# A two-layer trunk on one core: the block products' third phase leaves its chunks at once, and keys, values and queries of layer 1 change places

## The chip, the cores and the metric

One Trainium2 chip, one of its cores. The engines are TensorE (PE; its weight loads are PEld), VectorE (DVE), ScalarE (ACT), GpSimd (POOL) and SyncE (SP), which issues nearly all DMA transfers. The metric is the device time of one execution in microseconds; the profile is of one execution, and its own time stands beside its span below.

## The reference

`x` is 512 x 1024 in fp32, `mem` 256 x 1024. Two layers; each is a mixer, a cross-attention into `mem` with 4 heads of 256, and a gated feed-forward of width 2816 with a causal convolution of width 3. After each of the six steps stands x <- LayerNorm(alpha x + f(x)).

```
for layer in range(2):
    mix = mixer_ab(x, ...) if layer == 0 else mixer_c(x, ...)
    x = layer_norm(alpha * x + mix, ...)
    x = layer_norm(alpha * x + cross_attend(x, mem, wq, wkv, wo), ...)
    x = layer_norm(alpha * x + conv_ffn(x, w_up, conv_w, conv_b, w_down), ...)
```

Layer 0's mixer is a gated half (gelu, a norm, a 128 x 128 mixing of positions) beside a pooling half; layer 1's is `W_out(B * conv3(C * W_in x))`.

## The kernel before

**Numbers.** All matmuls work on fp32 split in two parts: `split` (lines 84 to 87) writes the rounded copy `h` with an ACT cast (L86) and the rest `l` with a DVE subtraction (L87), and `mm3` (226 to 228) multiplies h by h, h by l and l by h into one PSUM bank. A matmul has 128 x 128 stationary and up to 512 moving columns.

**Weights.** `plan` is the list of all weight tiles in the order of use. `Weights.load` fetches up to three tiles ahead with DMAs on SP (L149 or L186) and splits the oldest into a ring of five (`wh`, `wl`); `weights.done()` frees a tile and loads the next, so where `done` stands in the program sets when a load is issued and when its cast and subtraction come in ACT's and DVE's queues. `take` demands the plan's order.

**Activations.** `x` lies as four row blocks of 128 positions (`x0` to `x3`). `to_feat` turns one row block with eight transposes (L366) and splits it into `xT`, the form that the next projection needs. `proj_batch` multiplies several weights with `xT`; given `late`, it computes columns 0 to 255 of all weights first, calls `late` ahead of the last weight (the turning of row blocks 2 and 3), and then columns 256 to 511.

**Block products.** The products that end the mixers (`ab_w_out`, `c_w_out`) and the feed-forwards (`ffn_w_down`, five of its six groups) use seven block products in place of eight, on 2 x 2 blocks of both sides (`Blocks`, `fast_product`, lines 370 to 454). POOL forms the sums of weight blocks (L162, L169 to L171). The first phase multiplies A11, A12 and S1, the second S2 and S4, the third S3 (onto the bank X) and A22 (bank Z). Between them DVE adds the banks to the row blocks of `x` (L381) and PE goes on into the same banks, so a matmul of the next phase waits for the add before it. In the last group the statistics (L486) and the norms (`normalise`, L336 to L341, with a power on POOL, L338) stand between. In the third phase the order is A22 of half 0, S3 of half 0, S3 of half 1, A22 of half 1; its weights are freed only in half 1.

**Around.** The last product before a use of `mem` calls `prepare`: the norm's rows, the slots of the next `xT`, and with `ahead` the loading and splitting of `mem` (`load_mem`, L91). The keys (`proj_k`) come next, beside the norms: whole in layer 0, with the turning of row blocks 0, 1 ahead of head 2 and 2, 3 ahead of head 3. In layer 1 heads 0 and 1 come ahead of `mixer_c`, heads 2 and 3 after `c_w_out`. `attend` then computes the queries (four weights at once, then one each), loads `mem` again, and interleaves scores (softmax: L701 to L711), values and turned probabilities (L719). The tiles for all of it come from a ring of 12 (`act`).

The order of each engine's queue is not the program's alone: a scheduler places instructions within it. The listings below show that order.

Of the kernel before, what the change touches and what calls it, by code (L numbers as in the profile page):

```python
# [20 lines left out]
HEADS = 4  # L21
# [16 lines left out]
def kernel(ctx: ExitStack, tc: tile.TileContext, a: dict, out: bass.AP):  # L38
    nc = tc.nc
# [73 lines left out]
    for layer in range(2):  # L113
        if layer == 0:
            plan += [("ab_w_v", i) for i in range(4)] + [("ab_w_f", i) for i in range(4)] + [("pool_w",)]
            plan += [("ab_w_f", i) for i in range(4, 8)]
            plan += fast_plan("ab_w_out", 0, 0, 4)
            plan += [("xa_wk", layer, i) for i in range(8)]
        else:
            plan += [("xa_wk", layer, i) for i in range(4)]  # L120
            plan += [("c_w_in", i) for i in range(24)]
            plan += fast_plan("c_w_out", 0, 0, 4)
            plan += [("xa_wk", layer, i) for i in range(4, 8)]
        plan += [("xa_wq", layer, i) for i in range(8)]
        plan += [("xa_wv", layer, n, i) for n in range(2) for i in range(4)]
# [244 lines left out]
    def fast_product(act, name, layer, i0, first, norm=None):  # L370

        halves = (0, 1)
        seen = set()

# [51 lines left out]
        for p in halves:  # L428
            add(p, 1, X[p])
        for p in halves:  # L430
            add(p, 1, Y[p])
            stat(p, 1)
            if norm:
                norm[1](p)
        ts = [[weights.take(w, name, layer, i0 + i, i0 + top(i)) for i in firsts] for w in ("t3t3", "t4t4")]
        for p in halves:

            for k in (1, 0) if p == 0 else (0, 1):
                for i in range(n):
                    if k == 0:  # L440
                        mul(X, Blocks.S3, i, p, ts[0][i // 2], i % 2, True)
                    else:
                        mul(Z, Blocks.A22, i, p, ts[1][i // 2], i % 2)
                    if p and (i % 2 or i == n - 1):
                        weights.done()
                if k == 0:
                    add(p + 2, 1, X[p])
                    stat(p + 2, 1)
                    add(p + 2, 0, X[p])
                else:  # L450
                    add(p + 2, 0, Z[p])
            stat(p + 2, 0)
            if norm:
                norm[1](p + 2)

    def residual_norm(groups, wname, ln, layer, last=False, hooks={}, ahead=None):

# [7 lines left out]
        for gi, (make, k0, k1) in enumerate(groups):  # L465
# [25 lines left out]
            def prepare():  # L491
# [3 lines left out]
                if ahead:  # L495
                    ahead()

            if fast:
                fast_product(act, wname, wi, k0 // 2, gi == 0, (stat, norm, prepare))
                return xT, lambda: [to_feat(xT, t) for t in (0, 1)], lambda: [to_feat(xT, t) for t in (2, 3)]  # L500

            for n in range(2):
                if n == 0 or not final:
# [28 lines left out]
                    norm(t)  # L532
                weights.done(len(chunks))

        return xT, None, lambda: [to_feat(xT, t) for t in (2, 3)]


    def mixer_ab(xT):
# [61 lines left out]
        last = None  # L600
        for gi in range(4):
            (ps,) = proj_batch([("ab_w_f", 4 + gi)], xT)
            if gi < 2:
                pool_block(2 * gi)
                pool_block(2 * gi + 1)
            if gi == 1:
                weights.done()
            if last:
                gate_block(*last)
            ut = tmp()  # L610
            nc.scalar.activation(ut, ps, AF.Gelu_apprx_tanh)  # L611
            last = gi, ut
        gate_block(*last)
        return y
# [10 lines left out]
    def mixer_c(xT, late):  # L625
        y = Blocks()
        for m in range(KD):
            ps = proj_batch([("c_w_in", m * 3 + i) for i in range(3)], xT, late if m == 0 else None)
# [11 lines left out]
    def mem_at(t, i, k, c):  # L640
        return t[k // 4][i][:, (k % 4) * MEM + c.start : (k % 4) * MEM + c.stop]

    def proj_k(layer, mem, hooks={}, heads=range(HEADS)):
        full = slice(0, MEM)
        kT = [duo() for _ in heads[::2]]
        for h in heads:
# [10 lines left out]
            i = (h - heads[0]) // 2  # L657
            split(kT[i][0][:, c], kT[i][1][:, c], ps)
        return kT

    def proj_v(layer, mem, n):
        v = duo()
        ps = [ps_tile() for _ in range(2)]
        for k in range(KD):
            if k % 2 == 0:
# [12 lines left out]
    def attend(layer, xT, late, kT):  # L678

        q, o = Act(8), Act(8)  # L680
        for m0, m1 in ((0, 4), (4, 5), (5, 6), (6, 7), (7, 8)):
            ps = proj_batch([("xa_wq", layer, m) for m in range(m0, m1)], xT, late if m0 == 0 else None)
            for m in range(m0, m1):
                split(q.h(m), q.l(m), ps[m - m0])
        mem = load_mem()
        es, pT, v = {}, {}, {}

        def scores(h):
            es[h] = []
# [42 lines left out]
        scores(0)  # L732
        v[0] = proj_v(layer, mem, 0)
        turn(0)
        scores(1)
        values(0)
        v[1] = proj_v(layer, mem, 1)
        turn(1)
        scores(2)
        values(1)  # L740

        def second():
            turn(2)
# [36 lines left out]
        weights.load_beside(2 if k < 2 else 1, a["xT"][k], xT.tiles[k])  # L780
    weights.done(RING - 4)

    early = late = None
    mem = []

    def load_ahead():
        mem.append(load_mem())
# [1 line left out]
    for layer in range(2):  # L789
        if layer == 0:  # L790
            y = mixer_ab(xT)
            xT, early, late = residual_norm([(lambda: y, 0, 8)], "ab_w_out", "ln_mix", layer, ahead=load_ahead)
            kT = proj_k(layer, mem.pop(), {2: early, 3: late})
            late = None
        else:
            kT = proj_k(layer, mem.pop(), {1: early}, (0, 1))
            y = mixer_c(xT, late)
            xT, early, late = residual_norm([(lambda: y, 0, 8)], "c_w_out", "ln_mix", layer, ahead=load_ahead)
            kT += proj_k(layer, mem.pop(), {3: early}, (2, 3))
        o, hooks = attend(layer, xT, late, kT)  # L800
        xT, early, late = residual_norm([(lambda: o, 0, 8)], "xa_wo", "ln_xa", layer, hooks=hooks)
        up = [(lambda m0=m0, m1=m1, xT=xT, late=late: ffn_up(layer, xT, late, m0, m1), m0, m1) for m0, m1 in FFN_GROUPS[layer]]
        xT, early, late = residual_norm(up, "ffn_w_down", "ln_ffn", layer, layer == 1, ahead=None if layer else load_ahead)


# [73 lines left out]
```

## Time and profile before

| | |
|---|---|
| median of 3 runs | 1362.38 us (1360.58 to 1364.28) |
| the profiled execution's own time | 1363.97 us |
| its span, first to last instruction | 1362.2 us |
| mean granted TensorE clock | 0.989 of full |
| PE, DVE, ACT, POOL busy | 98%, 67%, 38%, 16% |
| DMA | 171.58 MB, mean 126 GB/s |

A matmul's row in the profile lasts from its start to the modelled end of its pipeline (389 ns at 512 columns), while the next starts sooner; how many start in a window tells the pace. A wait is put down to the instruction that released it last: `PE ps L226 <- DVE x L381` is time in which a matmul written on line 226 waited for a DVE instruction of line 381. The granted clock is that of TensorE in the window: 1.00 is full, 0.50 half.

### The profile page before, as it was taken

Reading aid. Unit: us, or ns where it says so; the run is one execution under the profiler, and the core shown is the slowest. Engines: PE = TensorE matmul, PEld = TensorE weight load, DVE = VectorE, ACT = ScalarE, POOL = GpSimd, SP = SyncE. Lnnn points to the kernel's source line nnn. Section 1 sums busy time; section 2 is a strip of 40 time slices with the busy share of each in tenths; the row PEclk is TensorE's granted clock in tenths of the full one; section 3 lists DMA queues with packets and bytes.
Section 4 is the critical chain, followed back from the end, with each engine's and each line's share of the span. In section 5 each row is a group of like instructions: output and inputs, shape, how many; then the busy total and the mean of one; then the engine's idle time right before and its main releaser. Section 6 shows DMA issues by size and latency. Waiting matters only on the chain. (4 is left out here: it accounts for less than half of the span.)

```text
span 1362.2 us, 16656 instructions
## 1 busy us (share of the span) xinstructions
PE 1328.3 (98%) x6541; PEld 1125.0 (83%) x6541; DVE 916.6 (67%) x1167; ACT 521.9 (38%) x667; POOL 217.2 (16%) x176
## 2 busy tenths in 40 slices
PE   9988999999999999999899999899999999999997
PEld 7867988888888888888888888888898888888886
DVE  6898746586676676579754579556577586577446
ACT  5443435324443443344333334245234334343330
POOL 1251000010240220142000151000010320141001
PEclk9989999999999999999899999899999999999998
DMA  8526634122354344236333335443123354236301
GB/s 312 162 93 203 214 111 151 48 78 85 101 171 131 93 133 160 86 105 213 124 109 100 101 124 189 153 138 111 61 78 102 100 185 124 88 114 218 107 0 62
DMA packets 50910, 171.58 MB, mean 126 GB/s; under 512 B 6032, under 2 KB 6160, under 8 KB 50832
## 3 DMA queue, kind: packets, MB, share of 16 engines
q1 hardware_dynamic: 49104, 164.23, 37.4%
q0 software_dynamic: 1728, 6.29, 1.3%
q8 instruction: 51, 0.84, 0.3%
q14 instruction: 27, 0.22, 0.0%
HBM read 168.40 MB, written 2.10 MB: 125 GB/s over the span
## 5 line engine op out<-in xcount | busy, mean ns | idle before, releaser
L87 DVE TENSOR_TENSOR wl<-raw,wh 128x1024 fp32r<-128x1024 f32 (+1 forms) x279 | 353.2, 1274 | 231.9 <-ACT wh L86 228.8
L228 PE MATMUL ps<-act,wl 128*128 128x512 f32 (+1 forms) x1340 | 484.5, 362 | 4.8 <-DVE wl L87 4.8
L226 PE MATMUL ps<-act,wh 128*128 128x512 f32 (+1 forms) x1340 | 484.6, 362 | 3.1 <-DVE rs L337 2.1
L227 PE MATMUL ps<-act,wh 128*128 128x512 f32 (+1 forms) x1340 | 484.6, 362 | 0.0
L86 ACT CAST wh<-raw 128x1024 fp32r<-128x1024 f32 (+1 forms) x279 | 290.0, 1042 | 480.7 <-PE ps L227 289.9
L228 PEld LDWEIGHTS ps<-act,wl 128*128 128x128 f32 x1340 | 255.3, 191 | 43.2 <-DVE wl L87 5.5
L226 PEld LDWEIGHTS ps<-act,wh 128*128 128x128 f32 x1340 | 255.1, 191 | 41.6 <-issue 2.3
L227 PEld LDWEIGHTS ps<-act,wh 128*128 128x128 f32 x1340 | 255.5, 191 | 37.8
L226 PE MATMUL ps<-wh,act 128*128 128x512 f32 (+1 forms) x656 | 257.6, 394 | 8.9 <-ACT tmp L611 4.6
L227 PE MATMUL ps<-wl,act 128*128 128x512 f32 (+1 forms) x656 | 255.3, 389 | 0.0
L228 PE MATMUL ps<-wh,act 128*128 128x512 f32 (+1 forms) x656 | 255.0, 389 | 0.0
L226 PEld LDWEIGHTS ps<-wh,act 128*128 128x128 f32 x656 | 124.4, 190 | 38.4 <-DVE x L381 5.7
L228 PEld LDWEIGHTS ps<-wh,act 128*128 128x128 f32 x656 | 123.9, 189 | 25.5
L227 PEld LDWEIGHTS ps<-wl,act 128*128 128x128 f32 x656 | 124.1, 189 | 25.0 <-DVE wl L87 0.2
L338 POOL TENSOR_TENSOR rs<-rs,mhalf 128x1 f32<-128x1 f32 x28 | 39.7, 1418 | 512.0 <-DVE rs L337 512.0
L162 POOL TENSOR_TENSOR raw<-raw,raw 128x512 f32<-128x512 f32 x27 | 38.6, 1431 | 454.7 <-DVE wl L87 376.9
L86 ACT CAST act<-ps 128x512 fp32r<-128x512 f32 x104 | 57.1, 591 | 84.8 <-PE ps L366 63.3
L87 DVE TENSOR_TENSOR act<-ps,act 128x512 fp32r<-128x512 f32 x104 | 67.8, 684 | 22.4 <-ACT act L86 22.4
L381 DVE SCALAR_TENSOR_TENSOR x<-x,ps 128x512 f32<-128x512 f32 x112 | 72.3, 676 | 10.4 <-PE ps L228 10.4
L87 DVE TENSOR_TENSOR act<-blocks,act 128x768 fp32r<-128x768 f32 (+1 forms) x54 | 71.8, 1341 | 10.6 <-ACT act L86 10.6
L86 ACT CAST act<-blocks 128x768 fp32r<-128x768 f32 (+1 forms) x54 | 48.9, 942 | 66.2 <-DVE blocks L277 66.2
L623 DVE SCALAR_TENSOR_TENSOR tmp<-ps,convw,tmp 128x511 f32<-128x511 f32 x88 | 65.6, 746 | 1.6
(80 smaller groups left out, 830.3 us busy)
## 6 DMA issues: line engine op xcount, KB each, us to landing
raw<-in_ffn_w_up SPq DMA_DIRECT2D x88, 512.0 KB, 3.7
raw<-in_ffn_w_down SPq DMA_DIRECT2D x63, 512.0 KB, 3.6
raw<-in_c_w_in SPq DMA_DIRECT2D x24, 512.0 KB, 3.6
raw<-in_xa_wk SPq DMA_DIRECT2D x16, 512.0 KB, 4.6
raw<-in_xa_wq SPq DMA_DIRECT2D x16, 512.0 KB, 4.3
raw<-in_xa_wv SPq DMA_DIRECT2D x16, 512.0 KB, 3.7
raw<-in_xa_wo SPq DMA_DIRECT2D x16, 512.0 KB, 4.4
raw<-in_ab_w_out SPq DMA_DIRECT2D x12, 512.0 KB, 3.8
```

The lines of the kernel that those rows point to most:

```text
L86: nc.scalar.copy(h, src)
L87: nc.vector.tensor_sub(l, src, h.bitcast(F32))
L162: nc.gpsimd.tensor_sub(both("t1"), w1[:, half[0]], w0[:, half[0]])
L226: nc.tensor.matmul(ps, lh, rh, start=start, stop=False, skip_group_check=more)
L227: nc.tensor.matmul(ps, lh, rl, start=False, stop=False, skip_group_check=more)
L228: nc.tensor.matmul(ps, ll, rh, start=False, stop=stop, skip_group_check=more)
L338: nc.gpsimd.tensor_tensor(rs, rs, mhalf, op=ALU.pow)
L381: nc.vector.scalar_tensor_tensor(z, z, scale, ps, op0=ALU.mult, op1=ALU.add)
L623: nc.vector.scalar_tensor_tensor(dst[:, s:], src[:, : S - s], tap(2 - s), dst[:, s:], op0=ALU.mult, op1=ALU.add)
```

## The change

The third phase of `fast_product` now runs S3 for both halves, chunk by chunk, and then A22; each chunk is freed as soon as it is used. The norm's callback has two parts: `ahead` (loading `mem`) is called before the second phase and the rows after it. The norms of row blocks 0 and 1 are called at the chunks of S3, that of block 2 at the end, and that of block 3 becomes the first of three hooks that the caller places. Layer 1 computes all four heads of keys ahead of `mixer_c` with these hooks at heads 1, 2 and 3; after `c_w_out` it computes the values (both halves) with the hooks in them, and `attend` begins with the queries, six of them, then scores(0), query 6, scores(1), query 7. Neither `c_w_in` nor the queries of layer 1 runs in halves any longer, and `mem` is loaded four times instead of five. In `mixer_ab` the gelu of a gate batch is written right after its projection.

```
-            plan += [("xa_wk", layer, i) for i in range(4)]
+            plan += [("xa_wk", layer, i) for i in range(8)]
...
         Z = [ps_tile() for _ in halves]
+        if norm:
+            norm[2]()
         for i in range(n):
             b = weights.take("t2b22", name, layer, i0 + i, i0 + i // 2 * 2, i0 + top(i // 2 * 2))
...
         if norm:
-            norm[2]()
+            norm[3]()
...
-            if norm:
-                norm[1](p)
-        ts = [[weights.take(w, name, layer, i0 + i, i0 + top(i)) for i in firsts] for w in ("t3t3", "t4t4")]
+        for i in firsts:
+            t3 = weights.take("t3t3", name, layer, i0 + i, i0 + top(i))
+            if norm and i < 4:
+                norm[1](i // 2)
+            for j in range(i, top(i)):
+                for p in halves:
+                    mul(X, Blocks.S3, j, p, t3, j - i, True)
+            weights.done()
+        for m in (1, 0):
+            for p in halves:
+                add(p + 2, m, X[p])
+                if m:
+                    stat(p + 2, 1)
+        for i in firsts:
+            t4 = weights.take("t4t4", name, layer, i0 + i, i0 + top(i))
+            for j in range(i, top(i)):
+                for p in halves:
+                    mul(Z, Blocks.A22, j, p, t4, j - i)
+            weights.done()
         for p in halves:
...
+            add(p + 2, 0, Z[p])
             stat(p + 2, 0)
-            if norm:
-                norm[1](p + 2)
+        if norm:
+            norm[1](2)
...
             (ps,) = proj_batch([("ab_w_f", 4 + gi)], xT)
+            ut = tmp()
+            nc.scalar.activation(ut, ps, AF.Gelu_apprx_tanh)
             if gi < 2:
...
-            ut = tmp()
-            nc.scalar.activation(ut, ps, AF.Gelu_apprx_tanh)
             last = gi, ut
...
+            for m in range(6):
+                queries(m, m + 1)
+            scores(0)
+            queries(6, 7)
+            scores(1)
+            queries(7, 8)
+            o = Act(8)
+            turn(0)
+            scores(2)
+            values(0)
+            turn(1)
+            values(1)
...
-            kT = proj_k(layer, mem.pop(), {1: early}, (0, 1))
-            y = mixer_c(xT, late)
...
-            kT += proj_k(layer, mem.pop(), {3: early}, (2, 3))
...
+            kT = proj_k(layer, mem.pop(), dict(zip((1, 2, 3), left)))
+            y = mixer_c(xT)
+            xT, left = residual_norm([(lambda: y, 0, 8)], "c_w_out", "ln_mix", layer, ahead=load_ahead)
+            v = {0: proj_v(layer, mem[0], 0, {4: left[0]}), 1: proj_v(layer, mem.pop(), 1, {0: left[1], 6: left[2]})}
+        o, hooks = attend(layer, xT, kT, v)
```

**ACT at the end of the first mixer.** `blocks` are the gate's blocks, written by DVE; the last L611 (L607 in the change) is the gelu of the last gate batch. Before:

```order
L86 CAST wh_714<-raw_577 128x1024
L611 ACTIVATE tmp_736<-ps_680 128x512
L86 CAST act_728<-blocks_676 128x768
L86 CAST act_733<-blocks_676 128x1024
L86 CAST wh_770<-raw_635 128x1024
L611 ACTIVATE tmp_783<-ps_738 128x512
```

And now:

```order
L86 CAST wh_714<-raw_577 128x1024
L607 ACTIVATE tmp_718<-ps_680 128x512
L86 CAST act_730<-blocks_678 128x768
L86 CAST act_735<-blocks_678 128x1024
L86 CAST wh_770<-raw_635 128x1024
L607 ACTIVATE tmp_774<-ps_738 128x512
```

The last gelu stands behind the same three casts in both.

**DVE from the first to the second phase of `ab_w_out`, layer 0.** `x_113` to `x_116` are the row blocks 0 to 3, `act_937` and `act_942` the two parts of `mem` (before, `act_1017` is the first of them), `wl` low halves of weights. Before:

```order
L381 SCALAR_TENSOR_TENSOR x_115<-x_115,ps_809 128x512
L87 TENSOR_TENSOR wl_918<-raw_862,wh_917 128x1024
L87 TENSOR_TENSOR wl_922<-row_709,wh_921 128x1024
L381 SCALAR_TENSOR_TENSOR x_116<-x_116,ps_810 128x512
L486 BN_STATS stats_803<-x_113 128x6
L486 BN_STATS stats_804<-x_114 128x6
L87 TENSOR_TENSOR wl_950<-row_835,wh_949 128x1024
L87 TENSOR_TENSOR act_1017<-raw_1015,act_1017 128x1024
L87 TENSOR_TENSOR wl_968<-raw_712,wh_967 128x1024
L381 SCALAR_TENSOR_TENSOR x_113<-x_113,ps_811 128x512
L87 TENSOR_TENSOR wl_986<-raw_838,wh_985 128x1024
L381 SCALAR_TENSOR_TENSOR x_114<-x_114,ps_812 128x512
```

And now:

```order
L382 SCALAR_TENSOR_TENSOR x_116<-x_116,ps_810 128x512
L87 TENSOR_TENSOR wl_918<-raw_862,wh_917 128x1024
L87 TENSOR_TENSOR wl_922<-row_709,wh_921 128x1024
L491 BN_STATS stats_803<-x_113 128x6
L491 BN_STATS stats_804<-x_114 128x6
L87 TENSOR_TENSOR act_937<-raw_935,act_937 128x1024
L87 TENSOR_TENSOR act_942<-raw_940,act_942 128x1024
L87 TENSOR_TENSOR wl_960<-row_835,wh_959 128x1024
L87 TENSOR_TENSOR wl_978<-raw_712,wh_977 128x1024
L382 SCALAR_TENSOR_TENSOR x_113<-x_113,ps_811 128x512
L87 TENSOR_TENSOR wl_996<-raw_838,wh_995 128x1024
L382 SCALAR_TENSOR_TENSOR x_114<-x_114,ps_812 128x512
```

The fourth row block's add moved ahead of two weights; both parts of `mem` now stand ahead of the adds of X (`ps_811`, `ps_812`), with the first weights of S3 and A22.

**ACT at the same place of the first feed-forward's last group.** `wh_4958` and `wh_4962` are weights of the second phase and of S3, `act_5058` and `act_5063` (now `act_4978` and `act_4983`) are `mem`. Before:

```order
L86 CAST wh_4936<-raw_4872 128x1024
L86 CAST wh_4958<-raw_4903 128x1024
L86 CAST wh_4962<-row_4784 128x1024
L86 CAST wh_4990<-row_4876 128x1024
L86 CAST act_5058<-raw_5056 128x1024
L86 CAST wh_5008<-raw_4787 128x1024
L86 CAST wh_5026<-raw_4879 128x1024
L86 CAST act_5063<-raw_5061 128x1024
```

And now:

```order
L86 CAST wh_4936<-raw_4872 128x1024
L86 CAST act_4978<-raw_4976 128x1024
L86 CAST act_4983<-raw_4981 128x1024
L86 CAST wh_4958<-raw_4903 128x1024
L86 CAST wh_4962<-row_4784 128x1024
L86 CAST wh_5000<-row_4876 128x1024
L86 CAST wh_5018<-raw_4787 128x1024
L86 CAST wh_5036<-raw_4879 128x1024
```

Both parts of `mem` moved ahead of the second phase's last weight and of S3's first.

More of the change, by code (lines that the diff above doesn't have):

```diff
@@ L119 @@
         else:
-            plan += [("xa_wk", layer, i) for i in range(4)]
+            plan += [("xa_wk", layer, i) for i in range(8)]
             plan += [("c_w_in", i) for i in range(24)]
             plan += fast_plan("c_w_out", 0, 0, 4)
-            plan += [("xa_wk", layer, i) for i in range(4, 8)]
-        plan += [("xa_wq", layer, i) for i in range(8)]
-        plan += [("xa_wv", layer, n, i) for n in range(2) for i in range(4)]
+        wq = [("xa_wq", layer, i) for i in range(8)]
+        wv = [("xa_wv", layer, n, i) for n in range(2) for i in range(4)]
+        plan += wv + wq if layer else wq + wv
         plan += [("xa_wo", layer, n, i) for n in range(2) for i in range(4)]
@@ L494, in prepare @@
                 xT = Wide(KD)
-                if ahead:
-                    ahead()
             if fast:
-                fast_product(act, wname, wi, k0 // 2, gi == 0, (stat, norm, prepare))
-                return xT, lambda: [to_feat(xT, t) for t in (0, 1)], lambda: [to_feat(xT, t) for t in (2, 3)]
+                fast_product(act, wname, wi, k0 // 2, gi == 0, (stat, norm, ahead or (lambda: None), rows))
+                return xT, (lambda: norm(3), lambda: [to_feat(xT, t) for t in (0, 1)], lambda: [to_feat(xT, t) for t in (2, 3)])
             for n in range(2):
@@ L533, in residual_norm @@
                 weights.done(len(chunks))
-        return xT, None, lambda: [to_feat(xT, t) for t in (2, 3)]
+        return xT, (lambda: [to_feat(xT, t) for t in (2, 3)],)
     def mixer_ab(xT):
@@ L623, in conv3, with mixer_c @@
             nc.vector.scalar_tensor_tensor(dst[:, s:], src[:, : S - s], tap(2 - s), dst[:, s:], op0=ALU.mult, op1=ALU.add)
-    def mixer_c(xT, late):
+    def mixer_c(xT):
         y = Blocks()
         for m in range(KD):
-            ps = proj_batch([("c_w_in", m * 3 + i) for i in range(3)], xT, late if m == 0 else None)
+            ps = proj_batch([("c_w_in", m * 3 + i) for i in range(3)], xT)
             p, cv = tmp(), tmp()
@@ L641, in mem_at, with proj_k @@
         return t[k // 4][i][:, (k % 4) * MEM + c.start : (k % 4) * MEM + c.stop]
-    def proj_k(layer, mem, hooks={}, heads=range(HEADS)):
+    def proj_k(layer, mem, hooks={}):
         full = slice(0, MEM)
-        kT = [duo() for _ in heads[::2]]
-        for h in heads:
+        kT = [duo() for _ in range(2)]
+        for h in range(HEADS):
             if h in hooks:
@@ L656, in proj_k, with proj_v @@
             c = slice((h % 2) * 512, (h % 2) * 512 + 512)
-            i = (h - heads[0]) // 2
-            split(kT[i][0][:, c], kT[i][1][:, c], ps)
+            split(kT[h // 2][0][:, c], kT[h // 2][1][:, c], ps)
         return kT
-    def proj_v(layer, mem, n):
+    def proj_v(layer, mem, n, hooks={}):
         v = duo()
@@ L664, in proj_v @@
         for k in range(KD):
+            if k in hooks:
+                hooks[k]()
             if k % 2 == 0:
@@ L676, in proj_v, with attend, queries @@
         return v
[L678 to L682, printed above, removed]
+    def attend(layer, xT, kT, v):
+        q = Act(8)
+        def queries(m0, m1):
+            ps = proj_batch([("xa_wq", layer, m) for m in range(m0, m1)], xT)
             for m in range(m0, m1):
                 split(q.h(m), q.l(m), ps[m - m0])
-        mem = load_mem()
-        es, pT, v = {}, {}, {}
+        es, pT = {}, {}
         def scores(h):
@@ L730, in values @@
                 split(o.h(2 * h + d), o.l(2 * h + d), ps)
[L732 to L740, printed above, removed]
+        if v is None:
+            for m in range(8):
+                queries(m, m + 1)
+            o, v, mem = Act(8), {}, load_mem()
+            scores(0)
+            v[0] = proj_v(layer, mem, 0)
+            turn(0)
+            scores(1)
+            values(0)
+            v[1] = proj_v(layer, mem, 1)
+            turn(1)
+            scores(2)
+            values(1)
+        else:
+            for m in range(6):
+                queries(m, m + 1)
+            scores(0)
+            queries(6, 7)
+            scores(1)
+            queries(7, 8)
+            o = Act(8)
+            turn(0)
+            scores(2)
+            values(0)
+            turn(1)
+            values(1)
         def second():
@@ L781 @@
     weights.done(RING - 4)
-    early = late = None
-    mem = []
+    mem, left = [], None
     def load_ahead():
@@ L791 @@
             y = mixer_ab(xT)
-            xT, early, late = residual_norm([(lambda: y, 0, 8)], "ab_w_out", "ln_mix", layer, ahead=load_ahead)
-            kT = proj_k(layer, mem.pop(), {2: early, 3: late})
-            late = None
-        else:
-            kT = proj_k(layer, mem.pop(), {1: early}, (0, 1))
-            y = mixer_c(xT, late)
-            xT, early, late = residual_norm([(lambda: y, 0, 8)], "c_w_out", "ln_mix", layer, ahead=load_ahead)
-            kT += proj_k(layer, mem.pop(), {3: early}, (2, 3))
[L800 to L803, printed above, removed]
+            xT, left = residual_norm([(lambda: y, 0, 8)], "ab_w_out", "ln_mix", layer, ahead=load_ahead)
+            kT = proj_k(layer, mem.pop(), dict(zip((1, 2, 3), left)))
+            v = None
+        else:
+            kT = proj_k(layer, mem.pop(), dict(zip((1, 2, 3), left)))
+            y = mixer_c(xT)
+            xT, left = residual_norm([(lambda: y, 0, 8)], "c_w_out", "ln_mix", layer, ahead=load_ahead)
+            v = {0: proj_v(layer, mem[0], 0, {4: left[0]}), 1: proj_v(layer, mem.pop(), 1, {0: left[1], 6: left[2]})}
+        o, hooks = attend(layer, xT, kT, v)
+        xT, left = residual_norm([(lambda: o, 0, 8)], "xa_wo", "ln_xa", layer, hooks=hooks)
+        up = [(lambda m0=m0, m1=m1, xT=xT, late=left[0]: ffn_up(layer, xT, late, m0, m1), m0, m1) for m0, m1 in FFN_GROUPS[layer]]
+        xT, left = residual_norm(up, "ffn_w_down", "ln_ffn", layer, layer == 1, ahead=None if layer else load_ahead)
 def _layout(inputs):
```

16 lines of the change are left out of this document (1 added, 15 removed).

## The prediction

> **What bounds the kernel now.** I read the page first, then the waits of the matmul engine, then windows cut along the steps of the granted clock.
>
> ```profile
> span 1362.2 us, 16656 instructions
> PE 1328.3 (98%) x6541; PEld 1125.0 (83%) x6541; DVE 916.6 (67%) x1167; ACT 521.9 (38%) x667; POOL 217.2 (16%) x176
> PE ps L228 <- DVE wl L87: 4.8, 3, 1.8
> PE ps L226 <- ACT tmp L611: 4.6, 1, 4.6
> PE ps L226 <- DVE x L381: 4.3, 8, 1.5
> PE ps L366 <- DVE act L87: 3.9, 4, 1.4
> PE ps L226 <- DVE rs L337: 2.1, 1, 2.1
> PE ps L366 <- DVE rs L337: 2.1, 1, 2.1
> ```
>
> TensorE sets the time: it is busy in 98% of the span and no other engine reaches 70%. So only two kinds of gain exist: fewer or cheaper matmuls, and fewer stalls of PE. The waits (line: total us, times, longest) name the stalls: a late low half of a weight (L87), the last gelu of the first mixer (L611), the residual adds of the block products (L381), and the norms with their turned copies (L337 and L366). The listed ones sum to 21.8 us. A stall has a second price, which the windows show (us, PE busy and instructions, granted clock, DMA share, GB/s):
>
> ```profile
> 81.75:85.16 3.41, 0.00 (x0) 1.00 0.83 303
> 85.16:88.58 3.42, 2.78 (x7) 0.50 0.01 2
> 88.58:91.99 3.41, 3.41 (x10) 0.50 0.06 10
> 102.23:105.64 3.41, 1.63 (x6) 1.00 0.83 290
> 129.53:132.94 3.41, 1.59 (x14) 1.00 0.01 2
> 132.94:136.36 3.42, 3.42 (x18) 0.50 0.65 182
> 136.36:139.77 3.41, 3.41 (x31) 1.00 0.31 125
> 658.60:662.00 3.40, 0.88 (x7) 1.00 0.81 299
> 662.00:665.40 3.40, 2.00 (x9) 0.50 0.44 160
> 665.40:668.85 3.45, 3.45 (x19) 0.50 0.22 33
> 839.50:842.90 3.40, 2.00 (x17) 1.00 0.00 0
> 853.15:856.56 3.41, 0.36 (x1) 1.00 0.84 297
> 856.56:859.97 3.41, 2.39 (x10) 0.50 0.76 253
> 859.97:863.40 3.43, 3.43 (x18) 0.50 0.87 220
> ```
>
> The clock moves in steps of 3.41 us. At full clock, a window with 1.59 us of work or less was followed by one at 0.50, one with 1.63 or 2.00 was not; at half clock, 2.00 and 2.39 kept it there. A full window at half clock does 18 matmuls of 256 columns where 136.36 to 139.77 does 31, so it costs 3.41 x 13/31 = 1.4 us; I count 1.5. Counted over starts of matmuls, loss sits in four places: the last gelu of the first mixer (about 8 us, with two half windows), the output product and keys of layer 0 (8.4), the end of the first feed-forward with keys and first batch of layer 1 (9.2), and the output product, keys and queries of layer 1 (10.0). In the last two, the stalls alone are about 6.
>
> **Half batches made whole: -2.2 us.** The first batch of c_w_in (3 weights) and of the queries of layer 1 (4) run in halves of 256 columns before. The change runs them whole: 168 pairs of 256-column matmuls become 168 of 512 columns.
>
> ```profile
> 674.00:684.00 10.00, 10.00 (x85) 1.00 0.16 54
> 690.00:750.00 60.00, 60.00 (x267) 1.00 0.30 93
> ```
>
> A window counts the matmul that hangs over its edge, so 85 in 10 us is 0.119 us each and 267 in 60 us is 0.2255. Two halves cost 0.238, a whole 0.2255, and 168 x 0.0125 = 2.1. The spacing of single starts (0.120 and 0.227) gives 2.2, which I take; counts off by one give 1.8 to 2.7.
>
> **Gelu ahead: 0.** The gelu of the last gate batch is written ahead of the gate work, but on ACT it still stands behind the two casts of the blocks, as the first order listing shows.
>
> ```profile
> 82.53 1.78 ACT L86 CAST act<-blocks 128x768 fp32r<-128x768 f32 x2 [4.52 <-DVE blocks L277]
> 85.16 0.59 ACT L611 ACTIVATE tmp<-ps 128x512 f32<-128x512 f32 x1
> ```
>
> ACT sat idle 4.52 us until the blocks came, while this gelu's input was long done, and PE waits for the gelu to free its bank. Nothing of that queue changes, so the 4.6 us wait and the two half windows stay. Bounds: 0.6 (the 0.59 us of one gelu) either way.
>
> **Memory split ahead, third phase by chunks.** memT's two loads now stand before the second phase, and their casts and subtractions stand ahead of the weights that the second phase still needs.
>
> ```profile
> 615.61 6.72 SPq L186 DMA_DIRECT2D raw<-in_xa_wk  x4
> 620.14 1.05 ACT L86 CAST wh<-raw 128x1024 fp32r<-128x1024 f32 x1 [3.18 <-POOL raw L170]
> 621.30 1.06 ACT L86 CAST wh<-row 128x1024 fp32r<-128x1024 f32 x1
> 623.00 1.21 DVE L87 TENSOR_TENSOR wl<-row,wh 128x1024 fp32r<-128x1024 f32 x1
> 624.13 0.67 DVE L381 SCALAR_TENSOR_TENSOR x<-x,ps 128x512 f32<-128x512 f32 x1
> raw<-in_xa_wk SPq DMA_DIRECT2D x2, 512.0 KB, 4.4
> ```
>
> At the end of the first feed-forward the slots that xa_wk's loads took from 615.61 become memT's. The first two of these took 4.4 us to land (the last row, over 615 to 619), the second issued about 617.7, so memT lands near 620.2 and 622.1. ACT waits for it: cast one, cast two from 622.1 to 623.1, the two weights to 625.2 instead of 622.4. DVE's subtractions follow and the fourth residual add ends near 627.1 instead of 624.8. PE waits there today 0.2 to 0.4 us; now about 2.6, **+2.3**. Queued behind it on DVE stand two statistics, memT's subtractions and two weights, then the adds of X that the third phase needs; PE is late by as much, so no second stall follows here. In return the keys of layer 1 run as four whole heads, 192 matmuls of 256 columns = 23 us, beside the last norms; the stalls at 645 to 648 and 658 to 665 and both half windows go, and about 0.8 us is left at the turning of the fourth row block. Loss 9.2 before, 3.4 to 3.5 after: **-5.7**.
>
> The same pattern stands at the output product of layer 1.
>
> ```profile
> 815.00 1.06 ACT L86 CAST wh<-raw 128x1024 fp32r<-128x1024 f32 x1 [4.08 <-POOL raw L170]
> 818.49 0.67 DVE L381 SCALAR_TENSOR_TENSOR x<-x,ps 128x512 f32<-128x512 f32 x1
> ```
>
> That add would end at 821.1 instead of 819.16, a stall of 2.6 instead of 0.8. The values (96 matmuls of 512 columns, 96 x 0.227 = 21.8 us) then cover the norms. What is late next is the turned copy of the fourth row block: its subtractions are queued behind three weights on DVE (1.21 us each), and the first query waits some 2.3. Loss 10.0 before, 5.3 after: **-4.7**.
>
> In layer 0 it is worse covered, since X's adds come sooner after.
>
> ```profile
> 101.63 2.10 SPq L186 DMA_DIRECT2D raw<-in_xa_wk  x4
> 102.00 1.05 ACT L86 CAST wh<-row 128x1024 fp32r<-128x1024 f32 x1 [0.23 <-PE ps L228]
> 107.86 0.67 DVE L381 SCALAR_TENSOR_TENSOR x<-x,ps 128x512 f32<-128x512 f32 x1
> raw<-in_xa_wk SPq DMA_DIRECT2D x4, 512.0 KB, 5.2
> ```
>
> memT takes the first two of the four issues at 101.63 and lands 3.6 to 4.7 us later (their median is 5.2). The casts end near 107.7 and the two weights near 109.7. DVE's list in the second order listing then gives: weights to 111.0, statistics to 112.3, memory to 114.6, two weights to 117.0, first X add to 117.6, one weight, second X add near 119.3. PE is ready for S3, which now comes first in the third phase, at 115.2: it waits 2 to 2.5 and then about 1.0. Before, A22 stood there and covered both adds; 6 matmuls per chunk of A22 (1.4 us) no longer do. Against that go the fourth add's 0.7 at 107.7, the stall and half window at 129.5 to 136.4, and 1.2 near 151. Loss 8.4 before, 6.1 after: **-2.3**.
>
> **Attention of layer 1: +1.7.** The order now ends turn(1), values(1), where scores(2), 24 matmuls or 2.9 us, stood between.
>
> ```profile
> L707 ACT ACTIVATE tmp<-ps,mx 128x256 f32<-128x256 f32 x32 | 14.8, 478 | 5.8 <-DVE mx L702 5.7
> L86 ACT CAST act<-ps 128x512 fp32r<-128x512 f32 x104 | 57.1, 591 | 84.8 <-PE ps L366 63.3 <-PE ps L228 21.4
> ```
>
> Values(0) with turn(1) take 12 x 0.227 + 8 x 0.11 = 3.6 us after scores(2). ACT in that time does a cast once half of values(0) is there (1.4 + 0.6), four exponentials (4 x 0.45 by their starts), a cast, and the cast that values(1) needs: 5.0 and some handing over. PE waits 1.4 to 1.7; below, 0 if ACT takes the cast first.
>
> **The other four products: +0.3.** S3 first puts their X adds (0.67 us) on the edge of the path; each gains or loses up to 0.3. One memT load and split fewer lies beside matmuls: 0.
>
> Sum: -2.2 + 0 - 2.3 - 5.7 - 4.7 + 1.7 + 0.3 = -12.9 without half windows. Four new stalls of 2.3 to 3.5 us can each starve a window. A stall of 2.6 leaves a window at most 1.6 us of work in 7 of 10 positions against the 3.41 us grid ((3.41 + 2.6 - 2 x 1.8)/3.41). So two to three half windows at 1.5 add about 4: **-9**. The profiled run took 1363.97 us, 1.8 more than its span and 1.6 more than the median, so the sum gives 1355 for that run and 1353.4 against the median of 1362.38.
>
> The Trainium skill ("TensorE: Matmul & The Clock Gate", Part 1) says that the clock falls back after about one whole idle window of 3.4 us. By that rule no new stall would cost clock and the time would be 1349.5. This trace disagrees: the window from 129.53 still held 1.59 us of work, and the next ran at 0.50.
>
> **Rivals.**
> 1. The waits only move. Each of the three products also gets two half windows after its stall, as 658 to 669 shows, and the first queries get one: 7 x 1.5 = 10.5 on -12.9, 1360. For it: 0.88 us of work, in a window with pauses on both sides of a short burst, brought two. Against: the new stalls come as one pause.
> 2. Slower: memT comes late. ACT takes its casts in order, so each us that memT lands later moves three products. Landings here run from 3.5 to 6.6 us. Say each pair lands d later, and the stalls of 2.6 + d then empty a whole window and bring two half windows each (+3.0): -12.9 + 3(d + 3.0) is a loss of 0.3% (4.1 us) from d = 2.7. At d = 3 it is +5.1, 1367.5. DMA share 0.83 in the windows beside speaks for late landings, the 4.4 us for xa_wk in the same slots against.
> 3. No wait at the adds: memT lands before ACT needs it. Then 2 x 2.3 and 3 us go from the sum with their half windows: about 1342.
> 4. The gelu does get ahead: 4.6 + 3.0 more, 1345.8. The order speaks against it.
> 5. The change doesn't do what it says: norms and turned copies still hold up the first query and first batch, only the halves and layer 0's part are left, 1358 to 1359.
>
> **How the numbers follow.** Forecast, with 2 or 3 half windows, 1350 to 1357: 0.66. Rival 1: 0.12, rival 2: 0.04, rival 3: 0.07, rival 4: 0.04, rival 5: 0.07. About 0.3%, 4.1 us, is what a measurement can tell from no change, so faster means below 1358.3. The forecast, rivals 3 and 4, and about half of rivals 5 and 1 are faster: 0.85; same 0.10; slower 0.05. The range 1345 to 1360 leaves out rivals 2 and 3 and parts of 1.
>
> **What the changed profile would show.** The waits L337 at the first batch and first query are gone; the wait for L611 is still 4.6 us; the waits for the residual adds grow to some 9 us in all, with one of 2 to 3 us in each of the three products; a new one of 1.5 us at the end of layer 1's values. PE has 168 instructions fewer. Wrong would be: no residual add above 1 us (rival 3), or a wait above 4 us at one with memT ahead of it on ACT (rival 2).

## The result and the profile after

The changed kernel takes 1351.72 us, the median of 4 runs (1350.42 to 1352.94), against 1363.09 for the kernel before beside it. The ratio is 0.9919 (95% interval 0.9900 to 0.9938); on a second chip, beside other kernels, it was 0.9901 (0.9882 to 0.9921). So it is 0.8 to 1.0% faster, 11 to 13 us. The profiled execution took 1352.71 us, with a span of 1350.9.

The page of the changed kernel, and then its waits of PE (line: total us, times, longest):

```profile
span 1350.9 us, 16327 instructions
...
PE 1321.7 (98%) x6373; PEld 1110.2 (82%) x6373; DVE 915.6 (68%) x1165; ACT 519.5 (38%) x665; POOL 219.9 (16%) x176
```

```profile
PE ps L226 <- DVE x L382: 10.3, 8, 3.1
PE ps L226 <- ACT tmp L607: 4.6, 1, 4.6
PE ps L226 <- ACT act L86: 1.2, 1, 1.2
...
PE ps L226 <- DVE act L87: 0.7, 1, 0.7
PE ps L226 <- DVE tmp L595: 0.4, 1, 0.4
PE ps L366 <- DVE act L87: 0.3, 1, 0.3
```

PE has 168 instructions less and is still 98% busy. The waits for a weight's low half (4.8 us) and for the norms (2.1 and 2.1) are gone, those for turned copies fell from 3.9 to 0.3. The waits for the residual adds (now line 382) grew from 4.3 to 10.3, one of 1.2 us is new at the end of layer 1's values, and the gelu's 4.6 us stayed.

Where the time went is seen when each start of a matmul is compared with the spacing of undisturbed ones (0.2267 us at 512 columns, 0.120 at 256, 0.109 at 128) and the excess summed by stretch:

| stretch (times of the kernel before) | before | after | forecast, half windows apart |
|---|---|---|---|
| first mixer's end, 78 to 99 | 7.9 | 7.4 | 7.9 |
| output product and keys of layer 0, 99 to 160 | 8.4 | 7.0 | 6.1 |
| last product of the first feed-forward to first batch of layer 1, 600 to 690 | 9.2 | 5.4 | 3.5 |
| output product, values, queries of layer 1, 800 to 890 | 10.1 | 4.6 | 5.3 |
| attention of layer 1, 890 to 1000 | 0.2 | 1.8 | 1.9 |
| the other four products | 1.6 | 2.5 | 1.9 |
| all of the span | 40.3 | 31.2 | |

The excess fell by 9.2 us and the span by 11.3; the 2.1 between them is what 168 whole matmuls cost less than 336 halves at these spacings.

The windows of the granted clock, after the change, on the grid of its own changes (at 103.27, 106.69, 625.51 and 628.92, whole multiples of 3.413 us apart; us, PE busy, clock, DMA share, GB/s):

```profile
622.10:625.51 3.41, 0.88 (x4) 1.00 0.76 244
625.51:628.92 3.41, 3.41 (x10) 0.50 0.70 232
820.07:823.49 3.42, 2.76 (x13) 1.00 0.73 253
823.49:826.90 3.41, 1.77 (x8) 1.00 0.73 229
826.90:830.31 3.41, 3.41 (x17) 1.00 0.78 267
```

Two stalls of nearly one length, 2.7 and 2.5 us. The first lies inside one window, leaves 0.88 us of work in it, and the next window runs at half clock. The second is cut by a border, the worse of its windows still has 1.77, and the clock stays. The Trainium skill ("TensorE: Matmul & The Clock Gate", Part 1) asks for an idle window of 3.4 us before the clock falls; 0.88 us of work did not prevent it here.

### The profile page after: what moved, and what is told of

It reads as the page before. It is cut to its first block, busy times and chain, and to the rows that moved or that the text cites. A ratio compares the mean times of both kernels' runs of the same rounds, so it can differ in the third digit from the quotient of the medians.

```text
span 1350.9 us, 16327 instructions
## 1 busy us (share of the span) xinstructions
PE 1321.7 (98%) x6373; PEld 1110.2 (82%) x6373; DVE 915.6 (68%) x1165; ACT 519.5 (38%) x665; POOL 219.9 (16%) x176
## 5 line engine op out<-in xcount | busy, mean ns | idle before, releaser
L226 PE MATMUL ps<-act,wh 128*128 128x512 f32 (+1 forms) x1284 | 473.1, 369 | 0.8 <-DVE act L87 0.7
L227 PE MATMUL ps<-act,wh 128*128 128x512 f32 (+1 forms) x1284 | 473.0, 368 | 0.1
L228 PE MATMUL ps<-act,wl 128*128 128x512 f32 (+1 forms) x1284 | 472.9, 368 | 0.0
L226 PEld LDWEIGHTS ps<-act,wh 128*128 128x128 f32 x1284 | 242.1, 189 | 41.8 <-DVE act L87 1.9
L227 PEld LDWEIGHTS ps<-act,wh 128*128 128x128 f32 x1284 | 242.2, 189 | 40.3 <-DVE act L87 0.4
L228 PEld LDWEIGHTS ps<-act,wl 128*128 128x128 f32 x1284 | 242.2, 189 | 39.8
L226 PE MATMUL ps<-wh,act 128*128 128x512 f32 (+1 forms) x656 | 258.4, 395 | 15.3 <-DVE x L382 10.3
L228 PE MATMUL ps<-wh,act 128*128 128x512 f32 (+1 forms) x656 | 256.2, 391 | 0.0
L228 PEld LDWEIGHTS ps<-wh,act 128*128 128x128 f32 x656 | 124.4, 190 | 26.0
L338 POOL TENSOR_TENSOR rs<-rs,mhalf 128x1 f32<-128x1 f32 x28 | 43.1, 1539 | 483.0 <-DVE rs L337 483.0
```

Source lines behind the costliest of these rows:

```text
L226: nc.tensor.matmul(ps, lh, rh, start=start, stop=False, skip_group_check=more)
L227: nc.tensor.matmul(ps, lh, rl, start=False, stop=False, skip_group_check=more)
L228: nc.tensor.matmul(ps, ll, rh, start=False, stop=stop, skip_group_check=more)
L338: nc.gpsimd.tensor_tensor(rs, rs, mhalf, op=ALU.pow)
```

## The experiments

My theory was the sum of the prediction: the moved work of layer 1 covers the norms, the chunks freed at once keep the keys' start free, and the price is that memT's casts, first in ACT's queue, hold up the fourth residual add. The rival that grew out of the first runs: VectorE's queue is the scarce thing in these stretches, so that what counts is whether it has something to do while PE waits. The runs were taken on three chips, with the kernel before beside them each time. A ratio is known to between 0.001 and 0.002, which is 1 to 3 us, so a difference of that size between two of them decides nothing by itself.

**memT after the second phase (e1).**

```
-        if norm:
-            norm[2]()
         for i in range(n):
             b = weights.take("t2b22", ...)
...
         if norm:
             norm[3]()
+            norm[2]()
```

> The changed kernel, with memT loaded and split after the second phase again, as before the change; everything else stays. My theory: memT's two casts on ACT, which wait for their data ahead of the second phase's last weight, make the waits at the fourth residual add (2.7 us at 624.8, 2.5 at 825.1) and part of the ones at S3 in layer 0 (0.6 and 0.9). These fall to 0.4, 0.8 and about 0.3, and the half window after 625 goes: 2.3 + 1.7 + 1.2 + 1.5 = 6 to 7 us less than the changed kernel, about 1345. Rival: it is the early memory that keeps the keys' start free, and with it late the waits of the keys for a weight's low half (1.98, 1.74, 1.57 us before the change) come back: then the two cancel, 1351 to 1354, with PE waiting at L228 for DVE L87 at the start of the keys.

Measured: 0.9937 of the kernel before (0.9921 to 0.9954), 2 to 5 us above the changed kernel (0.9901 and 0.9919 in its two measurements). The waits of PE in it:

```profile
PE ps L226 <- DVE x L382: 6.6, 10, 3.0
PE ps L366 <- DVE act L87: 5.9, 3, 2.7
```

The two waits for the fourth add shrank as my theory said, from 2.7 and 2.5 to 0.4 and 0.7 us, and still the kernel was slower: nearly 3 us each are lost in front of the transposes beside the keys of both layers, and 1.8 at the first query. That is neither my theory nor the wait that its rival named (L228 at the keys). VectorE's busy time points to a reason. In the kernel before, in the changed one and in e1, in this order (us, DVE busy and instructions, clock, DMA share, GB/s):

```profile
622.00:640.00 18.00, 14.87 (x20) 1.00 0.77 265
640.00:668.00 28.00, 28.00 (x38) 0.89 0.39 131
```

```profile
622.00:640.00 18.00, 16.28 (x21) 0.91 0.78 262
640.00:668.00 28.00, 27.56 (x38) 1.00 0.50 152
```

```profile
622.00:640.00 18.00, 14.07 (x18) 1.00 0.74 251
640.00:668.00 28.00, 27.56 (x38) 1.00 0.55 171
```

From 640 to 668, the stretch of the norms, VectorE is full, or all but full, in all three. In the 18 us ahead of it, it idles 3.1 us before the change, 1.7 in the changed kernel and 3.9 in e1. My reading: work on memory done there fills VectorE time that would be lost, so what PE pays at the add it gets back at the transposes. These rows alone do not prove it. Taken from 606 on, the three idle 3.2, 4.0 and 4.2 us, since VectorE in the changed kernel stands still 2.25 us ahead of the fourth add. And from 600 to 690 the excess in e1 is 5.2 us, against 5.4 and 3.0 in the two profiles of the changed kernel. The clear loss lies in layer 0, from 99 to 160: 9.7 against 7.0 and 5.0.

**The old third phase (e2).** In the changed kernel, A22 of half 0 again goes first, and the chunks are freed in half 1; the norms of row blocks 0 and 1 stand ahead of the phase, and that of block 3 stays with the caller.

```
-        for i in firsts:
-            t3 = weights.take("t3t3", ...)
...
+        ts = [[weights.take(w, ...) for i in firsts] for w in ("t3t3", "t4t4")]
+        for p in halves:
+            for k in (1, 0) if p == 0 else (0, 1):
...
+                    if p and (i % 2 or i == n - 1):
+                        weights.done()
```

> The changed kernel with the third phase in the old order (A22 of half 0, S3 of both halves, A22 of half 1, weights freed in the second half only); memT stays early, keys, values and queries stay moved. My theory: freeing the chunks at once is what took away the waits of the keys for a weight's low half (1.98, 1.74, 1.57 us), so with the old order they come back, and with them at least one half window (1.5): +5 to +7; the waits at S3 (0.6 and 0.9 in layer 0, 1.0 in the last block product) go: -2.5. Sum +3 to +4.5, about 1355.5. Rival: the keys' start was freed by the early memory and the moved norms, not by the chunks; then only the gain is left, 1349.

Measured: 0.9893 (0.9876 to 0.9909), as fast as the changed kernel or 1 to 3 us faster. The waits at S3 in layer 0 are gone, the keys wait 0.7 us once for a low half, and none of the three waits of 1.6 to 2 us came back:

```profile
PE ps L226 <- DVE x L382: 8.0, 6, 2.6
...
PE ps L226 <- ACT wh L86: 0.5, 1, 0.5
PE ps L228 <- DVE wl L87: 0.5, 1, 0.5
```

The rival holds: leaving the chunks at once, the part that gives the change its name, brings no gain that these runs can tell.

**Both undone (e9).** The old third phase and memory after the second phase, so that of the change the moved keys, values and queries, the whole batches and the gelu are left.

> The changed kernel with both parts of the block product undone: memT after the second phase and the old third phase. What is left of the change is the moved keys, values and queries of layer 1, the whole batches and the gelu. If the memory and the third phase matter only through VectorE's queue, which is full in these stretches whatever the order, the moved work of layer 1 carries most of the gain: the waits at 645 to 665 and 840 to 858 of the kernel before shrink anyway, and layer 0 is as before the change (8.4 us lost from 99 to 160). Then 4 to 7 us above the changed kernel and 5 to 8 below the kernel before. Rival: early memory and early freeing are needed for the moved keys and values, and without both the keys wait for a weight's low half as before: then within 3 us of the kernel before.

Measured: 0.9937 (0.9922 to 0.9952), against 0.9901 for the changed kernel beside it (e10 below). So the moved work of layer 1, with the whole batches and one loading of `mem` less, carries 8 to 9 us, the early memory 3 to 6, and the third phase none that can be told: e1 and e9, which differ by it alone, have the same ratio. The waits for a low half do come back here, as the rival said, though the time does not:

```profile
PE ps L228 <- DVE wl L87: 3.4, 2, 2.1
PE ps L366 <- DVE act L87: 3.2, 2, 1.6
PE ps L227 <- DVE wl L87: 2.2, 1, 2.2
```

With early memory they are gone, or small (0.5 us in e2, 1.4 in e12), in either order of the third phase. With late memory and chunks freed at once (e1) they are gone too, but there PE loses 5.9 us in front of the turned copies instead of 3.2. So either part alone takes these waits away, and the chunks do it without making the kernel faster.

**The changed kernel again (e10)**, as the base for e9, e8 and e7.

> The changed kernel itself, on this chip beside the others, as the base of their differences. All theories: a ratio to the kernel before of 0.990 to 0.994, as measured first; the residual adds still hold PE for some 10 us and two to three half windows follow, not always at the same stall.

Measured: 0.9901 (0.9882 to 0.9921). The waits for the adds came to 8.8 us. The half windows in layer 0 and after the first feed-forward's add (1.9 us here) did not come, while PE waited 3.3 us for the add in layer 1 and two half windows followed, from 821.90 to 828.73.

**Early memory alone (e6).** In the kernel before, only the loading and splitting of memT moves ahead of the second phase.

```
         Z = [ps_tile() for _ in halves]
+        if norm:
+            norm[3]()
...
                 xT = Wide(KD)
-                if ahead:
-                    ahead()
```

> The kernel before with one part of the change alone: memT is loaded and split ahead of the second phase. Theory of the prediction: the fourth add waits 2.5 to 3 us at the end of the first feed-forward and at the output product of layer 1, 4 us more in all with up to two half windows, and nothing is won, 3 to 6 us slower than before. Rival, after e1, e2 and e9: VectorE is the full queue in the stretch of the norms, and work that it does while PE waits for the adds is work less there; then the waits at 645 to 665 and 840 to 858 shrink by 2.4 us each and it comes out within 2 us of before.

Measured: 0.9978 (0.9969 to 0.9988), 2.8 us faster. What the prediction took for a price comes out as a gain. The adds wait about as priced (2.5 and 2.7 us), but the norms and weights give back more:

```profile
PE ps L226 <- DVE x L381: 8.0, 7, 2.6
PE ps L366 <- DVE act L87: 4.8, 4, 1.4
...
PE ps L366 <- DVE rs L337: 0.9, 1, 0.9
PE ps L226 <- DVE rs L337: 0.9, 1, 0.9
PE ps L228 <- DVE wl L87: 0.5, 1, 0.5
```

Before, these were 4.3, 3.9, 2.1, 2.1 and 4.8. By stretch, the excess fell from 8.4 to 6.4 us in layer 0 (99 to 160) and from 9.2 to 8.0 at the end of the first feed-forward; at the output product of layer 1 it did not fall (10.1 and 10.3).

**Memory's subtractions on GpSimd (e8).** As e1, and:

```
     def load_mem():
...
-            nc.vector.tensor_sub(l, src, h.bitcast(F32))
+            nc.gpsimd.tensor_sub(l, raw, h.bitcast(F32))
```

> The changed kernel with memT after the second phase (as in e1) and its two subtractions on GpSimd instead of VectorE. Theory: VectorE's queue is what e1 lost to (waits of 2.8, 2.9 and 1.8 us for the turned copies); with 2 x 1.2 us less in it at each of the three places these waits fall to about 0.5, and the residual adds stay quick: 1345 to 1347 on the first chip's scale, 5 us below the changed kernel. Rival: GpSimd slows VectorE while it runs (subtractions of 1.2 us take 2.3 beside it in the trace), so that nothing is won: the waits stay above 2 us and the time stays at e1's, 2 to 3 us above the changed kernel.

Measured: 0.9951 (0.9936 to 0.9966), no faster than e1 (0.9937). The waits for turned copies fell only from 5.9 to 4.9 us, and those for the adds grew from 6.6 to 7.8. GpSimd's two pieces and VectorE's two beside them:

```profile
628.20 2.41 POOL L646 TENSOR_TENSOR act<-raw,act 128x1024 fp32r<-128x1024 f32 x1 [3.92 <-ACT act L645]
...
635.48 2.40 POOL L646 TENSOR_TENSOR act<-raw,act 128x1024 fp32r<-128x1024 f32 x1 [4.34 <-ACT act L645]
```

```profile
629.10 2.60 DVE L87 TENSOR_TENSOR wl<-raw,wh 128x1024 fp32r<-128x1024 f32 x1 [1.75 <-ACT wh L86]
...
636.37 2.59 DVE L87 TENSOR_TENSOR wl<-raw,wh 128x1024 fp32r<-128x1024 f32 x1 [1.16 <-ACT wh L86]
```

A subtraction that takes 1.22 us alone took 2.60: it began 0.9 us after GpSimd's and ended 1.1 us after it, about its own length. Nothing left VectorE's time, as the rival said. The Trainium skill ("SBUF — State Buffer", "SBUF: two separate sides") tells of a port pair that GpSimd and a VectorE instruction with two SBUF inputs lock against each other for whole instructions; these four rows agree.

**turn(1) ahead of scores(2) (e3).**

```
             turn(0)
+            turn(1)
             scores(2)
             values(0)
-            turn(1)
             values(1)
```

> The changed kernel with turn(1) ahead of scores(2) in layer 1's attention, so that the cast of the turned probabilities stands ahead of the four exponentials on ACT. My theory: the 1.39 us wait of values(1) goes, nothing else moves: 1350.3. Rival: the values wait for ACT anyway, since the exponentials then hold the cast of values(0) that frees its bank; then the wait shows at another matmul and the time stays at 1351.7.

Measured: 0.9880 (0.9866 to 0.9895). The wait of 1.39 us is gone and the attention loses 0.2 us as before the change, so the mechanism stands. The time fell by 3 to 5 us, more than the 1.4: the profile shows one half window less, the one at 103 in layer 0, where nothing was changed.

**The gelu freed (e4).** The second gate block is written after the fourth gelu.

```
-            if last:
-                gate_block(*last)
-            last = gi, ut
+            if gi in (1, 3):
+                for args in left:
+                    gate_block(*args)
+                left = []
+            left.append((gi, ut))
```

> The changed kernel with the second gate block written after the fourth gelu, so that this gelu has no cast of gate blocks ahead of it on ACT. My theory: the wait of 4.6 us at 80.8 is queue order on ACT, so it goes with its half window (1.5): 1345 to 1346. Rival: DVE, full in 78 to 92, sets the pace there; the blocks of the gate come as much later as the gelu comes sooner, and PE waits for the last blocks in the first phase of the output product instead: 1349 to 1353, with a wait of several us for DVE L87 or ACT L86 on blocks.

Measured: 0.9885 (0.9870 to 0.9900). The wait for the gelu is gone from the list; others stand in its place:

```profile
PE ps L226 <- ACT act L86: 6.2, 2, 5.0
...
PE ps L226 <- DVE tmp L595: 1.7, 1, 1.7
PE ps L228 <- DVE act L87: 1.6, 2, 1.0
```

From 78 to 160 us the excess is 13.9, against 14.4 and 13.5 in the two profiles of the changed kernel. So the rival: VectorE sets the pace there (busy 20.9 of 21.0 us from 78 to 99 in this run). The time that it gained beside the changed kernel lies elsewhere, where it has no half window (its two are at 97 to 104), so the cause of that part is not shown to be the edit.

**Old third phase and turn(1) early (e7).**

> The changed kernel with the old third phase (e2) and turn(1) ahead of scores(2) (e3). The two lie 70 us apart and share no queue's work, so they should add: 1.4 for the turn and 1 for the third phase, 2 to 3 us below the changed kernel, the spread of the half windows (1.5 each) on top. If e2's gain was chance alone, 1.4.

Measured: 0.9883 (0.9867 to 0.9899), 3.3 us below the changed kernel's median beside it, as it should be if the two add. But e3 alone has 0.9880, so that the third phase's order adds anything to turn(1) is not shown.

**The adds first (e11).** The last two weights of each first phase are split after the six residual adds are written.

```
                 for p in halves:
                     mul(Y, Blocks.S1, j, p, t1, j - i)
-                weights.done()
-            weights.done()
+                if j < n - 1:
+                    weights.done()
+            if top(i) < n:
+                weights.done()
...
             add(p + 2, 1, Y[p])
+        weights.done(2)
```

> The changed kernel, with the last two weights of each first phase split only after the six residual adds are written, so that the fourth add has no low half ahead of it on VectorE; memT stays early. Theory: the wait of PE for the fourth add (2.7 and 2.5 us, the largest that the change brought) is there only because two low halves, whose casts stand behind memT's on ACT, stand ahead of the add; it falls to about 0.4 to 0.8, and with it about one half window: 4 to 5 us below the changed kernel, a ratio near 0.987. Rival: VectorE is full, and the two low halves come later by what the add gains; then a wait of 1 to 2 us shows at the second phase's last chunk or at S3, and the ratio stays within 0.002 of the changed kernel's 0.990 to 0.992.

Measured: 0.9859 (0.9844 to 0.9874), 1344.37 us, 6 to 8 us below the changed kernel. At the first feed-forward's last product of the changed kernel, ACT's casts of memT wait for their data:

```profile
617.26 1.05 ACT L86 CAST act<-raw 128x1024 fp32r<-128x1024 f32 x1 [2.68 <-DMA raw<-in_memT]
619.77 1.05 ACT L86 CAST act<-raw 128x1024 fp32r<-128x1024 f32 x1 [1.47 <-DMA raw<-in_memT]
```

VectorE at the same place, in the changed kernel and then here:

```profile
616.49 3.07 DVE L382 SCALAR_TENSOR_TENSOR x<-x,ps 128x512 f32<-128x512 f32 x5
621.80 1.23 DVE L87 TENSOR_TENSOR wl<-raw,wh 128x1024 fp32r<-128x1024 f32 x1 [2.25 <-ACT wh L86]
622.94 1.22 DVE L87 TENSOR_TENSOR wl<-row,wh 128x1024 fp32r<-128x1024 f32 x1
624.08 0.68 DVE L382 SCALAR_TENSOR_TENSOR x<-x,ps 128x512 f32<-128x512 f32 x1
```

```profile
616.80 3.66 DVE L382 SCALAR_TENSOR_TENSOR x<-x,ps 128x512 f32<-128x512 f32 x6
621.67 1.22 DVE L87 TENSOR_TENSOR wl<-raw,wh 128x1024 fp32r<-128x1024 f32 x1 [1.21 <-ACT wh L86]
622.81 1.22 DVE L87 TENSOR_TENSOR wl<-row,wh 128x1024 fp32r<-128x1024 f32 x1
```

Here six adds stand in one row; in the changed kernel it is five, a gap of 2.25 us, two subtractions and then the sixth, which is the fourth row block's. The waits for the fourth add (2.7 and 2.5 us) are gone in all products, the 0.4 to 1.0 us in the other four too; in exchange PE waits 0.6 and 0.9 at S3 here and 0.3 and 0.9 in layer 1. By stretch, the excess fell by 3.6 us at the end of the first feed-forward, by 2.1 at the output product of layer 1 and by some 2.5 in the other four products; in layer 0, where the add stood ahead of the two weights already, it did not fall (7.0 and 7.1). Both sides were part right: the theory in the gain and its cause, the rival in that some of it comes back.

**All three (e12), and with the gelu (e13).**

> e7 (old third phase, turn(1) early) with e11's edit. If the edits add: e7's 0.9883 less 4 to 5 us, about 0.985. If the rival of e11 holds: 0.988.

> e12 with the second gate block after the fourth gelu (e4). In e4 the two stretches from 78 to 160 us together lost 0.4 us less than in the changed kernel, so within 1 us of e12; with the fourth add freed, the wait for the blocks' casts (5.2 us in e4) stays, since it stands ahead of the adds.

Measured: e12 0.9852 (0.9835 to 0.9868), 1343.30 us, 20 us below the kernel before and 7 to 9 below the changed one; e13 0.9855 (0.9840 to 0.9870). The two cannot be told from each other or from e11; in e13 PE still waits 3.9 us for the blocks' casts. e12's waits of PE:

```profile
PE ps L226 <- ACT tmp L608: 4.6, 1, 4.6
PE ps L226 <- DVE x L382: 2.3, 1, 2.3
PE ps L366 <- DVE act L87: 1.2, 2, 0.6
...
PE ps L226 <- DVE act L87: 0.9, 1, 0.9
PE ps L228 <- DVE wl L87: 0.9, 2, 0.5
```

The old third phase gives A22's cover back to the adds that S3 needs: the waits at S3 that e11 had are gone.

## Why the prediction was right, and where its reasons were not

The forecast was 1353.4, within 1345 to 1360; 1351.7 was measured, the forecast -9 and the measured -11.4 against the kernel before.

**Sizes that held.** The whole batches: 2.1 against 2.2, both counted with the same spacings, so that this tests the count alone. The gelu: its wait of 4.6 us stayed, behind the same casts. The fourth add: 2.7 and 2.5 against 2.6 and 2.6. Attention: 1.4 against 1.4 to 1.7, and e3 shows that its cause was the order on ACT. Half windows: two new ones (after 103 and after 625) against two to three; that at 103 follows the adds of the first phase, which the sum had not listed, so this agreement is partly luck. Two half windows follow the gelu in both kernels, but after the change the first of them (82.79 to 86.21) lies almost wholly in the stall, so that matmuls ran at half clock for 3.0 us instead of 5.5. In e10, e11 and e12, with the same gelu, it is 3.8 to 5.1 us: that depends on where the border falls.

**Sizes that did not.** S3 in layer 0 was to wait 2 to 2.5 and 1.0 and waited 0.6 and 0.9 (1.1 and 0.9 in e10). The step that failed is the meeting of two times: VectorE's list put the end of the first X add at 117.6 and it came at 116.6, and PE, which was to be ready at 115.2, came at 116.2, behind the half window at 103. In turn the adds of the first phase made PE wait 3.2 us in one piece from 100.4 to 103.8, as much as the three waits of 1.7, 0.8 and 0.7 before; the sum had struck out the 0.7. That the stretch as a whole came near its forecast (7.0 with a half window of about 1.4, against 6.1 without) is luck: two of its terms were wrong in opposite directions. The first queries waited 1.6 (0.9 and two steps of 0.4) against 2.3. The other four products lost 0.9 more than before, not 0.3; 0.7 of it came in the last, where PE lost 1.0 us (0.5 in e10) at an add of the first phase, and not at S3, where the forecast had put it.

**Reasons that fell.** Two steps had the right sum with wrong parts. "Memory split ahead" was booked as a price, 2.3 us in the first feed-forward and 1.8 in layer 1, and the gain of these stretches went to the moved keys and values. The waits were sized well, but e6 gives the early split alone a gain of 2.8 us, and e1 and e9 lose 2 to 6 without it. The sum followed PE's waits one by one and never asked which engine was full behind them. And the keys' waits for a low half, which the expectation of e2 put down to chunks kept too long, go with either part of the block product alone (e1, e2) and come back only without both (e9).

Of the rivals, number 1 is half true: the waits did move to the adds (6.0 us more of them), but two half windows came with them, not seven. Number 3 (no wait at the adds) named the right place for more: 1342, where e11 came out at 1344 by taking that wait away, though by another order on VectorE and not by an earlier memT. Number 2 found no support: the second cast of memT began at 619.8, 2.4 us ahead of the old clock, so at 622.2 on it, where the forecast had 622.1. Nor did number 5: the waits for the norms (L337) are gone. Number 4 was blocked by the queue, and where e4 removed the block, by VectorE.

Open: where a half window falls differs between executions of one kernel, and so 1 to 3 us in a comparison of two profiles can be chance. That early memory gains because it fills idle time of VectorE is my reading; e6, e9 and e1 show the gain, not its cause. The halves were not tried apart from the rest, and loading memT's data itself sooner was not tried.

## What to carry to other kernels

When a wait ends on one engine's queue, look at the busy share of that engine over the next 20 to 30 us: if it is full there, moving its work earlier can gain more than the wait that this makes costs (e6), and removing one wait may only move the loss (e1, e4). Then look at what stands ahead of a short instruction that PE needs (here a 0.68 us add behind two 1.2 us subtractions whose data was not there yet): writing the short one first gained 6 to 8 us (e11). Test each part of a change that has several: the part that named this one gave nothing that could be measured.

## What the runs showed of the hardware

A stall's price in clock depends on its place against a grid of 3.41 us: 2.7 us inside a window halved the next, 2.5 us across a border did not. In the fourteen traces of this case, between the warm-up and the end, every window at full clock with 1.59 us of PE work or less was followed by one at half, and every one with more than 1.80 by one at full; between these both occur (1.63 kept it, 1.70 did not). At half clock, 2.78 us of work or less kept the half and 2.85 or more ended it. A GpSimd subtraction of 2.4 us stretched a VectorE one from 1.22 to 2.60 us, so that moving work from one to the other freed nothing here.
